# New numbers and a wider tie for TensorE in the list scheduler of a four-layer diffusion transformer step

## The chip, the core and the metric

The kernel runs on one core of a Trainium2 chip. The metric is the device time of one execution in microseconds (us); lower is better.

## What is computed

One inference step of a diffusion backbone: four layers on 128 context tokens and 512 latent tokens of width 1024, all in float32. Each layer takes one mixer: global attention (layers 0 and 3), windowed attention with a sink logit (layer 1), two-dimensional neighbourhood attention with a learned bias (layer 2). The reference, cut to what matters:

```python
for l in range(DEPTH):
    # the context tokens alike, with c_ctx in place of c and no positions
    shift, scl, gate = modulation(c, w_mod[l], b_mod[l])      # silu(c) @ w_mod + b_mod, 3 x 1024
    u = rms_norm(h_lat, norm_pre[l]) * (1 + scl[:, None, :]) + shift[:, None, :]
    q, k, v, z = project(u, w_in[l], q_norm[l], k_norm[l])    # 1024 -> 2560, q and k normed per head
    k_ctx, v_ctx = cache_k[:, l], cache_v[:, l]
    if kind == 0:
        q, k = apply_rope(q, cos, sin), apply_rope(k, cos, sin)
        o = dense_attention(q, concat(k, k_ctx), concat(v, v_ctx), None)
    elif kind == 1:
        q, k = apply_rope(q, cos, sin), apply_rope(k, cos, sin)
        o = window_attention(q, k, v, k_ctx, v_ctx, sink)
    else:
        o = neighborhood_attention(q, k, v, k_ctx, v_ctx, na_rel_bias[l // N_MIXERS])
    h_lat = h_lat + gate[:, None, :] * rms_norm((o * silu(z)) @ w_out[l], norm_post[l])
```

There are 16 query heads of 64 and 4 key heads; the reference returns both streams and the context keys and values of every layer.

## The kernel before, in words

**How the order comes about.** The program does not write instructions in their final order. It first records operations in program order (`S.op`): each has the engines that may do it with an estimated duration in ns, the buffers that it reads and writes, and a priority, which is its index in the program plus a shift for its part (the table `ORDER`; the modulation has its own shift). `Sched.emit` then plays these operations through a model of the engines and emits them one by one. Engines have letters: P is TensorE, V VectorE (DVE), A ScalarE (ACT), G GpSimd (POOL), D the DMA queue on SyncE (SP). For each engine `emit` takes every recorded operation whose inputs have been emitted, works out when it could start, and keeps the one with the lowest key:

```python
t = max(x[3], free[e] + (self.TURN.get((last, x[2][3]), 0) if e == "P" else 0))
key = (max(t, free[e] + SLACK[e]), x[0])
```

Here `x[3]` is the time at which the inputs are there, `free[e]` the time at which the engine is done, `x[0]` the priority. All operations that can start within `SLACK` of the engine's end are a tie, and the priority decides between them. Of the engines' candidates the one that starts first is emitted. The tables only set the order; the chip then runs each engine's instructions in that order, with semaphores between engines.

**Kinds of work on TensorE.** `TURN` adds ns to an operation of one kind behind one of another kind. M are ordinary matmuls: the projections in pieces of three matmuls (`nat`, L456, `z_block`, L593, `nat_o`, L860) and the scores (L657, L683, L759). T are float32 transposes: of the normed input (`start_part`, L410), of probabilities (L732, L785), and the two small matmuls of the modulation's fold (`mod_part`, L349). R are transposes in the float32r type (`k_stack`, L512, for the keys, called ks below; `q_chunk`, L579). C are matmuls with 64 columns, probabilities times values (L739, L793), and before the change also the modulation's matmuls with 32 columns (`mod_part`, L342).

**The modulation.** The 3072 columns of each later layer's modulation are worked out in pieces of 256 columns while the layer before runs. A piece loads two halves of `w_mod` of 512 KB each (L336, buffers `wm`, of which there are three), runs eight matmuls (L342), has the result copied by ACT or DVE (L252), and folds it on TensorE (L349). A buffer with one slot (`cap_mod`) lets one piece be between these steps at a time.

**Weights.** The projections' weights come as tiles of 256 KB (L318, three `raw` buffers), which ACT copies to a rounded half (L257) and DVE or POOL subtracts to a rest half (L258) in one of eight `w` buffers. All loads, the modulation's among them, go through SP's queue in the order of `emit`; the output phase reads the residual (L897, 512 KB) there, and layer 2 its bias table (L624, 132.5 KB a head).

**Layers.** A layer runs keys and values, two halves of the queries, the gate path and attention; then its output phase (L860) with the norm, and for each block of 128 tokens the next layer's input: square sum, power on POOL, scaling, transposes (L410), scale and shift on DVE or ACT, and the split into two halves for the next layer's first projection (L456).

## Time and profile before

| | us |
|---|---|
| median of 3 runs | 1426.93 |
| lowest and highest run | 1423.52, 1427.0 |
| the profiled execution | 1422.92 |
| its span from the first instruction to the last | 1420.7 |
| TensorE busy in it | 1381.5 |
| VectorE, ScalarE, GpSimd busy | 955.9, 755.7, 274.7 |

The profiled execution is the faster end of the runs. The rows that the argument uses stand in a section of their own below. In them a start is in us from the span's start; a row of the timeline joins neighbouring instructions of one line and tile (xcount), its second column is what they were busy for together, and a bracket at its end is the idle time ahead of it with what released it. Matmuls overlap a little, so a row's busy time reaches past the next row's start; the distance between two starts is what a row held the engine for. A float32 matmul that is no transpose leaves two records, so the eight matmuls of a modulation are 16 in the trace and the two of its fold 4.

### The profile page before, as it was taken

To read this page: it belongs to the slowest core of one execution; us is meant where nothing else is said; L and a number is where in the kernel's file an instruction comes from. 1 tells how busy PE (TensorE), PEld (TensorE's weight loads), DVE (VectorE), ACT (ScalarE), POOL (GpSimd) and SP (SyncE) were. 2 spreads that over 40 slices of the span, in tenths; PEclk is the share of its full clock that TensorE was granted. 3 is DMA by queue.
4 is the path that set the end of the run, shared out by engine and by line. 5 is a ranking of instruction groups with operands and counts; after the bars stand their busy time and mean duration, and the time that the engine had idled before them with its cause. 6 is when DMAs were issued, how large, how long until landed. Compare 5 with 4: busy or idle time off the path is not lost.

```text
span 1420.7 us, 24387 instructions
## 1 busy us (share of the span) xinstructions
PE 1381.5 (97%) x8964; PEld 1119.1 (79%) x8964; DVE 955.9 (67%) x2334; ACT 755.7 (53%) x1858; POOL 274.7 (19%) x322
## 2 busy tenths in 40 slices
PE   6999999999999999999999999999999999999998
PEld 4687878887777888877777887787787887888876
DVE  5777667775586875887287577558368776578654
ACT  4455554555354665567245458358345455655541
POOL 1231013010032101101022443155022210221100
PEclk9999999999999999999999999999999999999999
DMA  8513032125442212224444212233443210110043
GB/s 326 180 49 119 1 116 73 51 87 196 149 143 90 89 50 100 72 84 147 156 149 146 94 54 94 67 119 121 145 160 115 67 60 16 60 54 7 3 148 126
DMA packets 61799, 145.05 MB, mean 102 GB/s; under 512 B 7472, under 2 KB 12656, under 8 KB 61680
## 3 DMA queue, kind: packets, MB, share of 16 engines
q1 hardware_dynamic: 61680, 143.49, 30.6%
q8 instruction: 71, 1.16, 0.4%
q14 instruction: 48, 0.39, 0.1%
HBM read 131.90 MB, written 11.57 MB: 101 GB/s over the span
## 4 chain that ended last, share of the span: by engine, by line
PE 81%; DMA 5%; DVE 5%; ACT 3%; issue 3%; POOL 2%; SPq 0%; DVEq 0%; POOLq 0%; ACTq 0%
PE B L456 18%; PE B L593 14%; PE B L739 9%; PE B L732 9%; PE S L860 7%; PE B L860 5%; PE S L657 5%; PE S L683 4%; PE B L342 3%; DMA raw<-in_w_in 3%; DMA raw<-in_w_out 2%; POOL sm L303 2%; PE S L456 1%; PE B L579 1%; DVE w L258 1%
## 5 line engine op out<-in xcount | busy, mean ns | idle before, releaser
L303 POOL TENSOR_TENSOR sm<-sm,mhalf 128x1 f32<-128x1 f32 (+2 forms) x100 | 117.5, 1179 | 551.9 <-DVE sm L310 282.3
L456 PE MATMUL B<-w,uB 128*128 128x512 f32 x816 | 208.8, 401 | 1.5 <-DVE uB L258 1.1
L257 ACT ACTIVATE w<-raw 128x512 fp32r<-128x512 f32 x224 | 136.7, 627 | 93.0 <-DMA raw<-in_w_in 44.6
L252 ACT ACTIVATE pt<-B 128x512 f32<-128x512 f32 (+1 forms) x221 | 121.9, 569 | 110.7 <-PE B L732 102.5
L456 PEld LDWEIGHTS B<-w,uB 128*128 128x128 f32 x816 | 148.7, 188 | 35.1 <-DVE uB L258 1.6
L593 PE MATMUL B<-uB,w 128*128 128x384 f32 x768 | 166.1, 347 | 0.0
L732 PE MATMUL B<-ident,p 128*128 128x128 f32 x1088 | 159.4, 278 | 2.5 <-ACT pt L252 1.1
L258 DVE TENSOR_TENSOR w<-raw,w 128x512 fp32r<-128x512 f32 x187 | 128.1, 695 | 46.9 <-ACT w L257 46.0
L732 PEld LDWEIGHTS B<-ident,p 128*128 128x128 f32 x1088 | 123.0, 141 | 36.8 <-issue 25.1
L739 PE MATMUL B<-pt,vt 128*64 128x256 f32 (+1 forms) x1152 | 143.3, 377 | 0.0
L456 PE MATMUL B<-w,uA 128*128 128x512 f32 x528 | 134.3, 402 | 1.2 <-ACT w L257 0.5
L593 PEld LDWEIGHTS B<-uB,w 128*128 128x128 f32 x768 | 129.9, 189 | 1.3 <-issue 0.8
L662 ACT ACTIVATE p<-S,sm 128x640 f32<-128x640 f32 x128 | 101.0, 792 | 54.0 <-DVE sm L660 47.6
L660 DVE TENSOR_REDUCE sm<-S 128x1 f32<-128x640 f32 x128 | 102.1, 818 | 28.4 <-PE S L657 27.7
L593 PE MATMUL B<-uA,w 128*128 128x256 f32 x768 | 116.6, 290 | 3.8 <-ACT pt L252 2.4
L456 PEld LDWEIGHTS B<-w,uA 128*128 128x128 f32 x528 | 96.5, 188 | 24.7 <-DVE w L258 1.5
L617 POOL TENSOR_SCALAR p<-p,sm 128x640 f32<-128x640 f32 (+2 forms) x63 | 46.2, 738 | 353.4 <-DVE sm L616 268.4
L739 PEld LDWEIGHTS B<-pt,vt 128*64 128x64 f32 x1152 | 72.6, 136 | 47.6 <-issue 17.7
L593 PEld LDWEIGHTS B<-uA,w 128*128 128x128 f32 x768 | 103.6, 191 | 7.2 <-ACT pt L252 2.6
L617 DVE TENSOR_SCALAR p<-p,sm 128x640 f32<-128x640 f32 (+2 forms) x193 | 95.5, 512 | 5.8
L657 PE MATMUL S<-kst,q 128*128 128x320 f32 x512 | 95.6, 319 | 0.6 <-ACT p L662 0.6
L696 ACT ACTIVATE p<-p,sm 128x512 f32<-128x512 f32 (+1 forms) x128 | 84.0, 659 | 10.1 <-DVE sm L694 8.9
(143 smaller groups left out, 2255.3 us busy)
## 6 DMA issues: line engine op xcount, KB each, us to landing
raw<-in_w_in SPq DMA_DIRECT2D x160, 256.0 KB
wm<-in_w_mod SPq DMA_DIRECT2D x80, 512.0 KB
raw<-in_w_out SPq DMA_DIRECT2D x64, 256.0 KB
w<-in_w_mod SPq DMA_DIRECT2D x16, 512.0 KB
xs<-q SPq DMA_DIRECT2D x15, 512.0 KB
q<-xs SPq DMA_DIRECT2D x15, 512.0 KB
q<-in_x SPq DMA_DIRECT2D x10, 512.0 KB
kst<-gs SPq DMA_DIRECT2D x8, 512.0 KB
```

The costliest lines, as they stand in the source:

```text
L252: alts = {"A": Ap(n, lambda e: e.activation(out(), in_(), AF.Copy)), "V": V(n, lambda e: e.tensor_copy(out(), in_()))}
L257: S.op([As(n, lambda e: e.activation(h(), src(), AF.Copy))], r, w)
L258: f = lambda e: e.tensor_sub(l(), src(), h().bitcast(F32))
L303: S.op([("G", 395 + 157 * n, lambda e: e.tensor_tensor(r.ap, v.ap, mhalf.ap.to_broadcast([128, n]), op=OP.pow), "pow")], r=[v, mhalf], w=[r])
L456: e.matmul(ps(), t.ap[:, s, k, off:off + 128], W[k].ap[:, w], start=k == 0 and i == 0, stop=k == 7 and i == 2)
L593: e.matmul(ps.ap[:, 0:w], W[k].ap[:, wi, 128 * f:128 * f + 128], t.ap[:, s, k, :], start=k == 0 and i == 0, stop=k == 7 and i == 2)
L617: f = lambda e, i=i, p=p, w=w: e.tensor_scalar(p.ap[:, 0:w], p.ap[:, 0:w], rs.ap[:, i:i + 1], 1.0, op0=OP.mult, op1=OP.mult)
L657: e.matmul(ps.ap[:, b, 0:320], Q[t + 1].ap[:, hh], kst.ap[:, g, s, 320 * b:320 * b + 320], start=s == 0, stop=s == 1)
L660: S.op([V(640, lambda e, ps=ps, i=i: e.tensor_reduce(negm.ap[:, i:i + 1], ps.ap[:, :, 0:320], axis=AX.XY, op=OP.max, negate=True))], r=[ps ...
L732: e.transpose(pt.ap[:, c:c + 128], p.ap[:, b:b + 128], ident.ap)
L739: e.matmul(po.ap[64 * x:64 * x + 64, 256 * half + q0:256 * half + q0 + w], vt.ap[:, kt, 64 * g:64 * g + 64], sbt.ap[:, c0:c0 + w], start=f ...
L860: e.matmul(ps(), t.ap[:, s, k, off:off + 128], W[k].ap[:, w], start=k == 0 and i == 0, stop=k == 7 and i == 2)
```

## The change

The table `TURN` gets other numbers and more pairs, and the tie on TensorE grows from 30 to 100 ns. The modulation's matmuls become a kind of their own, E, whose pairs are priced like those of C, with 76 ns between C and E. C behind C, 30 before, costs nothing. Four durations in the model change: 960 to 935 for the modulation's matmuls, 260 to 448 for its fold, and 300 to 336 for the two float32r transposes. The model's numbers change nothing but the order in which operations are emitted, and which engine is given an operation that may go to several.

```diff
--- before.py
+++ after.py
@@ -33,7 +33,7 @@
 WINDOW = 520
 PLAT = 270
 XLAT = 180
-SLACK = {'P': 30, 'V': 0, 'A': 220, 'G': 50, 'D': 80}
+SLACK = {'P': 100, 'V': 0, 'A': 220, 'G': 50, 'D': 80}
 DISLIKE = {'Ap': 1060, 'mada': 3020, 'G1': 980, 'mad': 900, 'V': 1260, 'V2': 960, 'G': 780}
 CAPS = {'p': 6, 'raw': 3, 'cap_prep': 3}
 NEG = -1e30
@@ -63,7 +63,11 @@
     LAT = {("P", "P"): 0, ("V", "V"): 130, ("A", "A"): 155, ("G", "G"): 110, ("P", "V"): 200, ("P", "A"): 200,
            ("G", "V"): 80, ("A", "V"): 110, ("V", "A"): 135, ("G", "A"): 150, ("D", "D"): 100, ("V", "P"): 235, ("A", "P"): 228}
 
-    TURN = {("C", "M"): 85, ("C", "T"): 30, ("C", "R"): 30, ("C", "C"): 30, ("R", "M"): 52, ("R", "C"): 52}
+
+
+    TURN = {("C", "M"): 179, ("E", "M"): 179, ("C", "T"): 132, ("E", "T"): 132, ("C", "R"): 132, ("E", "R"): 132, ("R", "M"): 45,
+            ("R", "C"): 110, ("R", "E"): 110, ("R", "T"): 45, ("T", "M"): 6, ("M", "C"): 88, ("M", "E"): 88, ("T", "C"): 94,
+            ("T", "E"): 94, ("C", "E"): 76, ("E", "C"): 76}
 
 
 
@@ -341,13 +345,13 @@
                 g = 32 * (k % 4)
                 e.matmul(ps.ap[g:g + 32, 0:256], cpad.ap[:, k, :], raws[k // 4].ap[:, k % 4], start=k < 4, stop=k >= 4,
                          skip_group_check=True)
-        S.op([P(960, mm, "C")], r=raws + [cpad], w=[ps], touch=[cap])
+        S.op([P(935, mm, "E")], r=raws + [cpad], w=[ps], touch=[cap])
         evac(256, lambda: pm.ap, lambda: ps.ap[:, 0:256], [ps], [pm])
 
         def fold(e):
             for x in range(2):
                 e.matmul(ps.ap[:, 2 * x:2 * x + 2], pm.ap[:, 128 * x:128 * x + 128], sel.ap, start=True, stop=True)
-        S.op([P(260, fold, "T")], r=[pm, sel], w=[ps], touch=[cap])
+        S.op([P(448, fold, "T")], r=[pm, sel], w=[ps], touch=[cap])
         S.op([V(4, lambda e: e.tensor_tensor(mc.ap[:, b:b + 2], ps.ap[:, 0:4].rearrange("p (b j) -> p b j", j=2),
                                              bc.ap[:, b:b + 2, None].to_broadcast([128, 2, 2]), op=OP.add))],
              r=[ps, bc], w=[(mc, b), (mc, b + 1)], touch=[cap])
@@ -510,7 +514,7 @@
                 for g in range(2):
                     c = 128 * (2 * i + g)
                     e.transpose(ps.ap[:, c:c + 128], hl.ap[:, i, g].rearrange("p a d -> p (a d)"), identr.ap)
-        S.op([P(300, tr, "R")], r=[hl, identr], w=[ps], touch=tc_)
+        S.op([P(336, tr, "R")], r=[hl, identr], w=[ps], touch=tc_)
         evac(512, lambda: kst.ap[:, :, :, 128 * COL[ct]:128 * COL[ct] + 128],
              lambda: ps.ap.bitcast(F32).rearrange("p (i g c) -> p g i c", i=2, g=2), [ps], [(kst, ct)])
 
@@ -577,7 +581,7 @@
                 def tr(e, hl=hl, pt=pt):
                     for h in range(4):
                         e.transpose(pt.ap[:, 128 * h:128 * h + 128], hl.ap[:, h], identr.ap)
-                S.op([P(300, tr, "R")], r=[hl, identr], w=[pt], touch=[cap])
+                S.op([P(336, tr, "R")], r=[hl, identr], w=[pt], touch=[cap])
                 evac(512, lambda i=i, q=q: q.ap[:, 4 * i:4 * i + 4].rearrange("p h t -> p (h t)"),
                      lambda pt=pt: pt.ap.bitcast(F32), [pt], [(q, i)])
             Q.append(q)
```

The lines after the table move down by four (L342 is L346 afterwards, L739 is L743).

TensorE at the boundary of layers 0 and 1 (L456 is the last projections of the key phase, L410 the transposes of the last block of tokens, L512 the keys' transposes, L342 and L349 the modulation). Before:

```order
L349 MATMUL B<-sel,pm 128x2 x2
L456 MATMUL B<-w,uB 128x512 x3
L512 MATMUL B<-identr,tmp 128x128 x4
L456 MATMUL B<-w,uB 128x512 x6
L410 MATMUL B<-ident,p 128x128 x8
L512 MATMUL B<-identr,tmp 128x128 x4
L456 MATMUL B<-w,uB 128x512 x3
L342 MATMUL B<-wm,cpad 32x256 x8
L349 MATMUL B<-sel,pm 128x2 x2
L456 MATMUL B<-w,uB 128x512 x24
```

After, in the same place:

```order
L516 MATMUL B<-identr,tmp 128x128 x4
L460 MATMUL B<-w,uB 128x512 x3
L516 MATMUL B<-identr,tmp 128x128 x4
L460 MATMUL B<-w,uB 128x512 x3
L346 MATMUL B<-wm,cpad 32x256 x8
L414 MATMUL B<-ident,p 128x128 x8
L353 MATMUL B<-sel,pm 128x2 x2
L516 MATMUL B<-identr,tmp 128x128 x4
L460 MATMUL B<-w,uB 128x512 x6
L516 MATMUL B<-identr,tmp 128x128 x4
L460 MATMUL B<-w,uB 128x512 x18
```

The modulation's eight matmuls, which stood behind the eight L410 transposes, now stand ahead of the same transposes (L414), three of the matmuls of L456 with them; behind the transposes a fold and one keys' transpose are left ahead of the long run of matmuls.

TensorE in the attention of layer 1, second half of the queries (L683 scores, L732 transposes of probabilities, L739 probabilities times values). Before:

```order
L739 MATMUL B<-pt,vt 64x256 x6
L739 MATMUL B<-pt,vt 64x128 x2
L732 MATMUL B<-ident,p 128x128 x4
L593 MATMUL B<-uB,w 128x384 x6
L683 MATMUL S<-kst,q 128x384 x2
L683 MATMUL S<-kst,q 128x512 x2
L683 MATMUL S<-kst,q 128x256 x4
L683 MATMUL S<-kst,q 128x384 x2
L732 MATMUL B<-ident,p 128x128 x14
L739 MATMUL B<-pt,vt 64x256 x6
L739 MATMUL B<-pt,vt 64x128 x2
L342 MATMUL B<-wm,cpad 32x256 x8
```

After:

```order
L743 MATMUL B<-pt,vt 64x256 x2
L743 MATMUL B<-pt,vt 64x128 x2
L346 MATMUL B<-wm,cpad 32x256 x8
L736 MATMUL B<-ident,p 128x128 x4
L687 MATMUL S<-kst,q 128x384 x2
L687 MATMUL S<-kst,q 128x512 x2
L736 MATMUL B<-ident,p 128x128 x7
L687 MATMUL S<-kst,q 128x256 x4
L687 MATMUL S<-kst,q 128x384 x2
L353 MATMUL B<-sel,pm 128x2 x2
L743 MATMUL B<-pt,vt 64x256 x4
L346 MATMUL B<-wm,cpad 32x256 x8
```

Before, a modulation stands at the end of the stretch behind a group of L739. After, two stand in it, each behind such a group, with 11 transposes, 10 score matmuls, a fold and four matmuls of L743 between them.

SP's queue at the boundary of layers 1 and 2 (raw<-in_w_out are tiles of the output projection, q<-xs the residual, tab the bias table of layer 2). Before:

```order
L318 DMA raw<-in_w_out 128x512 x3
L897 DMA q<-xs_4216 128x1x1024 x2
L318 DMA raw<-in_w_out 128x512 x2
L624 DMA tab<-in_na 128x1x265
L318 DMA raw<-in_w_in 128x512 x3
```

After:

```order
L322 DMA raw<-in_w_out 128x512 x3
L628 DMA tab<-in_na 128x1x265 x2
L901 DMA q<-xs_4225 128x1x1024
L322 DMA raw<-in_w_out 128x512 x2
L322 DMA raw<-in_w_in 128x512
L901 DMA q<-xs_4225 128x1x1024
L322 DMA raw<-in_w_in 128x512 x2
```

Two loads of the bias table and one of the residual now stand ahead of the last two tiles of the output projection, where two of the residual stood; the second residual load has moved behind them.

## Rows read from the trace of the kernel before

**Rows 1.** The page: busy time by engine, clock in 40 slices, chain by engine.

```profile
PE 1381.5 (97%) x8964; PEld 1119.1 (79%) x8964; DVE 955.9 (67%) x2334; ACT 755.7 (53%) x1858; POOL 274.7 (19%) x322
...
PEclk9999999999999999999999999999999999999999
...
PE 81%; DMA 5%; DVE 5%; ACT 3%; issue 3%; POOL 2%; SPq 0%; DVEq 0%; POOLq 0%; ACTq 0%
```

**Rows 2.** Timeline of PE, five places: start, busy us, engine, line, out<-in, shapes, count.

```profile
451.92 5.84 PE L456 MATMUL B<-w,uB 128*128 128x512 f32 x24
457.60 0.80 PE L579 MATMUL B<-identr,tmp 128*128 128x128 f32 x8
...
489.69 1.73 PE L739 MATMUL B<-pt,vt 128*64 128x256 f32 x16
491.36 0.65 PE L732 MATMUL B<-ident,p 128*128 128x128 f32 x4
...
637.49 0.87 PE L739 MATMUL B<-pt,vt 128*64 128x256 f32 x8
638.29 0.66 PE L732 MATMUL B<-ident,p 128*128 128x128 f32 x4
...
658.25 1.08 PE L739 MATMUL B<-pt,vt 128*64 128x256 f32 x8
659.26 0.55 PE L732 MATMUL B<-ident,p 128*128 128x128 f32 x3
...
1355.93 3.08 PE L860 MATMUL S<-w,uB 128*128 128x512 f32 x12
1358.94 0.66 PE L793 MATMUL B<-pt,vt 128*64 128x128 f32 x8
```

**Rows 3.** Timelines of SP (988.65) and PE (993.15) in layer 2.

```profile
988.65 0.39 SPq L336 DMA_DIRECT2D wm<-in_w_mod  x1
...
993.15 0.64 PE L342 MATMUL B<-wm,cpad 128*32 128x256 f32 x8 [0.26 <-DMA wm<-in_w_mod]
```

**Rows 4.** Timelines of SP and PE; windows (busy by engine, PEclk, DMA share, GB/s).

```profile
691.02 1.74 SPq L318 DMA_DIRECT2D raw<-in_w_out  x3
692.80 1.23 SPq L897 DMA_DIRECT2D q<-xs  x2
696.54 1.03 SPq L318 DMA_DIRECT2D raw<-in_w_out  x2
...
705.76 0.50 PE L860 MATMUL B<-w,uA 128*128 128x512 f32 x1 [2.42 <-ACT w L257]
706.49 5.08 PE L860 MATMUL B<-w,uA 128*128 128x512 f32 x14 [0.23 <-DVE w L258]
...
697.00:699.00 2.00, 1.87 (x7) 0.99 (x6) 0.77 (x3) 0.63 (x1) 0.00 (x0) 1.00 0.75 237
...
707.00:709.00 2.00, 2.00 (x6) 1.61 (x5) 0.05 (x1) 0.09 (x1) 0.00 (x0) 0.50 0.67 214
```

**Rows 5.** Timeline of PE at the first two boundaries between layers.

```profile
426.99 1.03 PE L410 MATMUL B<-ident,p 128*128 128x128 f32 x8
...
429.01 1.07 PE L342 MATMUL B<-wm,cpad 128*32 128x256 f32 x16
430.59 0.61 PE L349 MATMUL B<-sel,pm 128*128 128x2 f32 x4 [0.51 <-ACT pm L252]
431.05 2.11 PE L456 MATMUL B<-w,uB 128*128 128x512 f32 x8
...
763.28 1.07 PE L342 MATMUL B<-wm,cpad 128*32 128x256 f32 x16
```

**Rows 6.** Timeline of PE: waits in layers 0 and 2.

```profile
193.83 1.20 PE L512 MATMUL B<-identr,tmp 128*128 128x128 f32 x12 [1.12 <-ACT tmp L503]
...
884.72 0.66 PE L785 MATMUL B<-ident,p 128*128 128x128 f32 x4 [0.41 <-ACT pt L252]
...
887.62 0.96 PE L456 MATMUL B<-w,uA 128*128 128x512 f32 x3 [0.31 <-DVE tmp L469]
```

## The prediction

> **What bounds the kernel now.** First the busy times of the whole execution, the granted clock in 40 slices and the chain of waits [rows 1]: TensorE is busy for 1381.5 of 1420.7 us, so at most 39.2 us of the span is TensorE standing still, and the granted clock shows full speed in every slice. The chain that ended last goes through TensorE for 81%. So two things can move the time: what TensorE pays for its own work, and those 39 us. The pitch of the work shows that "busy" is not a trick of overlapping records: 24 matmuls of L456 in a row go from 451.92 to 457.60, 237 ns each, and that pitch recurs in every long run [rows 2]. The Trainium skill ("Perfetto Trace Analysis", section "Identifying the Most-Contended Engine") says that matmul busy share tells little of the headroom, and that the busy share of weight loads is the measure. That share is 79% here [rows 1]; by the rule a fifth of the span would be free, dearer or cheaper switches would be hidden, and the first term below would be 0, the sum -1.3. The pitch speaks against it, and I go by the pitch.
>
> **What the change does to the order.** The computation and the number of instructions on TensorE stay; the order moves. Counted over all rows of the two orders, TensorE enters a group of C or E matmuls (L739, L793, L342; neighbours counted as one group) 151 times before and 147 times after; runs of transposes fall from 285 to 268. More visible is where the E groups (modulation, L342) go. With the new table an E costs 76 ns behind a C, inside the tie of 100, while a transpose or an ordinary matmul costs 132 or 179 and falls out of it. So nearly every E is taken behind a C group as soon as its weights count as landed, up to 90 us earlier than before in the attention phases, and the ones left for the phases between layers become fewer. On SP the w_mod loads move with them, and at the second layer boundary other loads are exchanged.
>
> **Term 1, switches.** Two rows give a price. Twelve matmuls of L860 between two C groups take 3.01 us (1355.93 to 1358.94), twelve of L456 without one 2.84 (half of 5.68): 0.17 for leaving one C and entering the next [rows 2]. A C group's own time: 8 alone take 0.80 and 1.01 (637.49 to 638.29, 658.25 to 659.26), 16 together 1.67 (489.69 to 491.36), so joining two saves 0.14 [rows 2]. Together 0.31 us a group, against 0.22 to 0.27 in the table of the diff. Four groups fewer are -1.2 by the rows; all kinds of switches, count times the diff's numbers, give -1.07. I take **-1.1**, bounds -0.8 and -1.3. That is the whole direct gain: the count hardly falls, because entering a C (88) now also lies inside the tie.
>
> **Term 2, wider ties.** With a tie of 100 ns instead of 30, TensorE may be given an operation whose data come later although another stands ready. Run over the planner's choices this happens 20 times after and 9 before, so 11 more, each at most 100 ns: 0 to +1.1, I take **+0.5**, the middle.
>
> **Term 3, E behind its own load.** An E needs two 512 KB loads; three buffers exist, so the second load can only start when the E before it is done. At 988.65 SP issued such a second load amid weight loads, and the half of the E that needs it began at 993.15 after 0.26 idle: 4.5 us from issue to use [rows 3]. In the new order the distance from the E that frees the buffer to the E that needs it, priced with the start-to-start times of the same operations in this trace, is some 4.5 and 4.7 us in two places (the order of the attention phase of layer 1 shows the first) and 6.4 to 8 in six more; before, all but that one were 8.5 or more. The nearest row is the one at 988.65, a load of the same size in traffic: two waits of a quarter, **+0.5**. Lower bound 0; upper bound from the slowest landing in the rows, the loads issued at 696.54 whose tile is used at 705.76 [rows 4]: 9.2 us less the tile's conversion, which would be some 4 us of waiting at each of the two tightest: +8.
>
> **Term 4, the load that comes late at 705.** TensorE stands for 2.42 us at 705.76 on the ACT half of a w_out tile, and then runs at half clock (0.50, the 1.2 GHz level, from 707 to 709) [rows 4]. The 14 matmuls from 706.49 on are busy for 5.08 us, where 14 x 0.237 = 3.32 would do, and the one ahead of them holds the engine for 0.73 instead of 0.24: together 2.2 more, so the place costs 4.6. The two late loads were issued at 696.54 behind three of 256 KB and two of 512 KB: 1792 KB. In the new order one of the 512 KB loads stands behind them, and two of 132.5 KB in front: 1545 KB. At the 237 GB/s of 697 to 699 [rows 4] the 247 KB are 1.0 us. The wait would then be about 1.4 us, and a wait of 1.12 at 193.83 was not followed by the half clock [rows 6], so most of the 2.2 goes too: **-3.0**. Bounds 0 (the queue drains no earlier) and -4.6 (the place goes).
>
> **Term 5, fillers lost at the layer boundaries.** At 426.99 eight transposes start, whose result comes back through DVE for the matmuls at 431.05. Between them lie a ks transpose, three matmuls, an E (1.0 us with its half-microsecond wait behind it, 0.51 idle) and its fold, 0.46 [rows 5]. In the new order only a fold and a ks transpose stand there; the E comes 50 us later. If the way through DVE stays as long, the matmuls start when they did, and 1.0 + 0.46 of work is still owed. At the next boundary the same pattern holds one E of 1.0, at 763.28, which also goes. **+2.5**. Below: +1, if the three matmuls now ahead of the transposes fill time that was idle before them. Above: each of the two new waits comes near the 2.42 of term 4 and is followed by half clock for 2 us: +6.5.
>
> **Term 6, E in front of waits.** Several waits in the attention phases were TensorE arriving early: 1.12 at 193.83 (ACT), 0.41 at 884.72 and 0.31 at 887.62 [rows 6]. In front of each, two to four more E groups now stand, so TensorE arrives 3 to 5 us later while ACT and DVE get little new work: **-1.8**. Bounds -1.8 and 0, where the waits travel along because what they wait for also follows from TensorE's work.
>
> **Sum.** -1.1 + 0.5 + 0.5 - 3.0 + 2.5 - 1.8 = -2.4 us. The profiled execution took 1422.9 us (span 1420.7 and 2.2 around it), 4.0 below the median of the runs, 1426.93. Against its own time the sum gives 1420.5; set against the median, which the result will be compared with, 1424.5.
>
> **Rivals.** *Faster.* The wait at 705 goes with its half clock (-4.6), the early arrivals go and their smaller kin with them (-3), the boundaries lose one filler's worth (+1); with terms 1 and 2 (-0.6) that is -7.2, 1419.7. For it: all of these are short waits with an explanation in the order. Against it: freed waits on a shared ACT and DVE often reappear at the next exchange. *Slower by lost fillers.* Both boundary waits reach about 2 us, half clock follows each (+6.5), the 705 place stays as it is, term 6 gives 1: with the rest +5.4, 1432.3. It decides at the wait behind the eight transposes: waits of 1.12 left the clock alone, 2.42 did not. For it: the two new waits are estimated at just 2 us, and lost fillers are visible in the order. Against it: three matmuls have moved in front of the transposes and DVE may answer sooner. *Slower by late E weights.* If loads in traffic take 6.5 us instead of 4.5, the two tight places and those at 6.4 to 6.6 wait, some 4 us, and weight loads queued behind them on SP slip too: with +2 for that, some +5.5 on the rest without term 3's half, 1429 to 1433, 1432. *No effect.* If "busy by weight loads" were right or the waits simply change places, 1426.9.
>
> **How the numbers follow.** Forecast 0.33 (its own range 1422.6 to 1429); no effect 0.05; faster 0.34; slower by lost fillers 0.17; slower by late weights 0.11. A measurement of this kernel can tell about 0.3%, 4.3 us, from no change; so faster 0.34, same 0.38, slower 0.28. Faster and slower together hold more than half, so the range takes both in: 1417 leaves out the lower third of the faster case, 1434.5 the upper part of the slower ones.
>
> **What the profile after would show.** Term 1: L739 rows still in some 130 runs, E behind L739 in about two thirds. Term 3: waits of TensorE at L342 (now L346) on wm loads, under 1 us in all; several us mean the late-weights rival. Term 4: the wait of a w_out matmul at the second boundary under 1.5 us and no slice of half clock there. Term 5: idle time of about 2 us behind the L410 (now L414) transposes at two boundaries; a granted clock of 0.5 behind them is the fillers' rival. Term 6: no wait of over 0.5 us at the ks transposes near 194. The prediction is wrong if waits of TensorE on weight tiles (w from ACT or DVE) grow by several us in places that none of these terms names.

## The result and the profile after

The changed kernel is slower: a median of 1434.75 us over 5 runs (1432.86 to 1436.9), against 1426.93 over 5 runs of the kernel before (1423.52 to 1428.57). The ratio is 1.0070, with an interval from 1.0046 to 1.0093, so 7 to 13 us; the two medians are 7.8 apart. The forecast was 1424.5, and the end of its range, 1434.5, lies just below the result. The profiled execution is the one of 1434.75, with a span of 1433.0; the one of before had 1420.7, so there are 12.3 us to find between the two traces.

The page of the changed kernel, busy times and the chain that ended last, to be read against [rows 1]:

```profile
PE 1386.2 (97%) x8964; PEld 1122.6 (78%) x8964; DVE 963.4 (67%) x2340; ACT 756.0 (53%) x1855; POOL 268.0 (19%) x319
...
PE 80%; DVE 6%; DMA 6%; issue 4%; ACT 3%; POOL 1%; SPq 0%; DVEq 0%; POOLq 0%; ACTq 0%
```

The busy time of TensorE grew by 4.7 us though it has the same 8964 instructions, and its idle time from 39.2 to 46.8. Part of "busy" is half clock, so a finer account is needed. For it, each operation of TensorE is given the distance to the next one that the trace of before usually shows for its kind and the kinds of its neighbours; what a trace has beyond that is **standing or half clock**. It is an estimate, worked out from the two traces. By it the new order needs 1.1 us less in pure work, and 13.4 more of standing and half clock (62.1 against 48.7). Where it lies, in us, with the stretches in times of the trace of before (each begins and ends where both orders have issued the same work; the first 6 us are left out):

| stretch | before | after | after less before |
|---|---|---|---|
| 6 to 392: start, layer 0 | 23.4 | 21.7 | -1.7 |
| 392 to 496: first layer boundary | 2.7 | 4.3 | +1.6 |
| 496 to 665: layer 1 | 1.2 | 1.6 | +0.3 |
| 665 to 751: output phase of layer 1 | 8.7 | 11.4 | +2.7 |
| 751 to 825: second boundary, projections | 0.0 | 6.0 | +6.0 |
| 825 to 1005: layer 2 | 2.2 | 6.5 | +4.3 |
| 1005 to the end | 10.5 | 10.6 | +0.1 |

The traces say the same without any account. At places where both orders have issued exactly the same work on TensorE, the changed kernel is 2.1 us ahead at 392 and 0.7 ahead at 510, level at 724, and behind by 3.4 at 754, 8.3 at 825 and 12.0 at 1005.

TensorE between 695 and 772 in the changed kernel (timeline; a bracket is the idle time ahead and what ended it):

```profile
707.47 0.49 PE L864 MATMUL B<-w,uA 128*128 128x512 f32 x1 [3.03 <-ACT w L261]
708.20 4.98 PE L864 MATMUL B<-w,uA 128*128 128x512 f32 x14 [0.23 <-DVE w L262]
...
737.32 0.49 PE L460 MATMUL B<-w,uA 128*128 128x512 f32 x1 [3.42 <-ACT w L261]
...
757.05 0.52 PE L516 MATMUL B<-identr,tmp 128*128 128x128 f32 x4 [0.91 <-DVE tmp L426]
...
766.99 0.54 PE L516 MATMUL B<-identr,tmp 128*128 128x128 f32 x4 [0.68 <-DVE tmp L426]
...
769.53 2.08 PE L460 MATMUL B<-w,uB 128*128 128x512 f32 x4 [1.14 <-DVE uB L262]
```

The first wait is that of [rows 4], 3.03 instead of 2.42, again with 14 matmuls in 4.98 us behind it; between 510 and 724, where it lies, the two traces differ by no more than 0.7. The second is new: a tile of the next layer's w_in, 3.42. The three waits below are at the second boundary, where before had none of over 0.2 after 748.

SP and ACT of the changed kernel show how late the two tiles are: the issue on SP, and the conversion on ACT, which waits for the load.

```profile
693.27 1.73 SPq L322 DMA_DIRECT2D raw<-in_w_out  x3
695.05 1.30 SPq L628 DMA_DIRECT2D tab<-in_na  x2
696.39 0.58 SPq L901 DMA_DIRECT2D q<-xs  x1
698.79 0.99 SPq L322 DMA_DIRECT2D raw<-in_w_out  x2
...
726.29 0.61 SPq L922 DMA_DIRECT2D xs<-q  x1
...
728.07 4.01 SPq L322 DMA_DIRECT2D raw<-in_w_in  x3
...
706.79 1.28 ACT L261 ACTIVATE w<-raw 128x512 fp32r<-128x512 f32 x2 [7.79 <-DMA raw<-in_w_out]
...
736.64 1.67 ACT L261 ACTIVATE w<-raw 128x512 fp32r<-128x512 f32 x3 [6.66 <-DMA raw<-in_w_in]
```

The w_out tile issued at 698.79 is converted at 706.79, 8.0 us later; the w_in tile issued at 728.07 at 736.64, 8.6 us later. In the kernel before the same w_in tile was issued at 728.98, and ACT, which was busy with other work from 731.45 on, took it at 732.08.

### The profile page after: what moved, and what is told of

It reads as the page before. It is cut to its first block, busy times and chain, and to the rows that moved or that the text cites. A ratio compares the mean times of both kernels' runs of the same rounds, so it can differ in the third digit from the quotient of the medians.

```text
span 1433.0 us, 24375 instructions
## 1 busy us (share of the span) xinstructions
PE 1386.2 (97%) x8964; PEld 1122.6 (78%) x8964; DVE 963.4 (67%) x2340; ACT 756.0 (53%) x1855; POOL 268.0 (19%) x319
## 4 chain that ended last, share of the span: by engine, by line
PE 80%; DVE 6%; DMA 6%; issue 4%; ACT 3%; POOL 1%; SPq 0%; DVEq 0%; POOLq 0%; ACTq 0%
PE B L460 20%; PE B L597 13%; PE B L736 8%; PE B L743 8%; PE S L864 7%; PE B L864 5%; PE S L661 5%; PE S L687 3%; DMA raw<-in_w_in 3%; PE B L346 2%; DMA raw<-in_w_out 2%; PE B L583 2%; DVE w L262 1%; DVE tmp L426 1%; ACT w L261 1%
## 5 line engine op out<-in xcount | busy, mean ns | idle before, releaser
L256 ACT ACTIVATE pt<-B 128x512 f32<-128x512 f32 (+1 forms) x216 | 118.9, 567 | 102.0 <-PE B L736 98.1
L262 DVE TENSOR_TENSOR w<-raw,w 128x512 fp32r<-128x512 f32 x196 | 135.1, 700 | 52.9 <-ACT w L261 51.9
L743 PE MATMUL B<-pt,vt 128*64 128x256 f32 (+1 forms) x1152 | 144.0, 377 | 0.0
L666 ACT ACTIVATE p<-S,sm 128x640 f32<-128x640 f32 x128 | 101.2, 794 | 70.9 <-DVE sm L664 59.0
L621 POOL TENSOR_SCALAR p<-p,sm 128x640 f32<-128x640 f32 (+2 forms) x73 | 53.2, 735 | 397.3 <-DVE sm L620 282.8
L743 PEld LDWEIGHTS B<-pt,vt 128*64 128x64 f32 x1152 | 73.1, 136 | 46.3 <-issue 16.0
L621 DVE TENSOR_SCALAR p<-p,sm 128x640 f32<-128x640 f32 (+2 forms) x183 | 91.6, 515 | 5.1
L700 ACT ACTIVATE p<-p,sm 128x512 f32<-128x512 f32 (+1 forms) x128 | 84.0, 658 | 12.6 <-DVE sm L698 10.6
```

The lines of the kernel that those rows point to most:

```text
L256: alts = {"A": Ap(n, lambda e: e.activation(out(), in_(), AF.Copy)), "V": V(n, lambda e: e.tensor_copy(out(), in_()))}
L262: f = lambda e: e.tensor_sub(l(), src(), h().bitcast(F32))
L621: f = lambda e, i=i, p=p, w=w: e.tensor_scalar(p.ap[:, 0:w], p.ap[:, 0:w], rs.ap[:, i:i + 1], 1.0, op0=OP.mult, op1=OP.mult)
L743: e.matmul(po.ap[64 * x:64 * x + 64, 256 * half + q0:256 * half + q0 + w], vt.ap[:, kt, 64 * g:64 * g + 64], sbt.ap[:, c0:c0 + w], start=f ...
```

## Experiments

Ratios are against runs of the kernel before on the same chip; 0.001 is 1.43 us. Where an order is spliced or moved, the kernel replays a fixed list of operations, taken from the `emit` of one of the two kernels or of both, and the diff shows the list or the rows of one engine. An operation that the two orders have on different sides of a cut is fitted in so that each is issued once. Where two ratios from different chips are compared, their difference is known to some 0.002 to 0.003, 3 to 4 us; a smaller gain is one only if the trace shows it too.

### The second boundary, put in and taken out

```diff
-PLAN = before
+PLAN = before[:3229] + after[3229:3882] + before[3882:]
```

> The order of the kernel before, except the stretch of the second layer boundary (about 675 to 828 us), where the order of the changed kernel stands. Theory (the loss lies in what stands in this stretch: the wait of 3.03 for a w_out tile, the wait of 3.42 for a w_in tile with its half clock, the waits behind the L410 transposes; together +8.0 us between the two traces): 1426.9 + 8 = 1434.9. Rival (the stretch is only where a delay surfaces that the order ahead of it, in the attention of layer 1, has caused): about 1427, within 1.5.

Measured: 1432.89, ratio 1.0054 (1.0034 to 1.0074), 7.7 us. The theory stands: this stretch alone makes most of the loss. In the profiled execution, the fastest of the four, the wait for the w_in tile is 1.19 and not 3.42.

```diff
-PLAN = after
+PLAN = after[:3229] + before[3229:3882] + after[3882:]
```

> The mirror of it: the order of the changed kernel, except that stretch, where the order of the kernel before stands. Theory of the stretch: 1434.75 - 8 = 1426.7, with the second loss, in the attention of layer 2 (+4.1 between 828 and 1005 us), still there. Rival: about 1434.5, the waits appear at the same place in another order of the same work.

Measured: 1430.06, ratio 1.0025 (1.0007 to 1.0043), that is 6.4 us better than the changed kernel, nearer the theory's 8 than the rival's 0. But the wait for the w_out tile, which the order of before has too, was longer in the profiled execution, the slowest of ten, than in [rows 4], 5.25:

```profile
714.20 6.48 PE L864 MATMUL B<-w,uA 128*128 128x512 f32 x15 [5.25 <-ACT w L261]
```

So a late load is no fixed number: with the same rows of SP ahead of it the tile took 8.5 us from issue to conversion in the kernel before and 10.2 here (703.28 to 713.52). The rest of the longer wait is TensorE's, which has 1.1 us less to do between issue and wait than in the kernel before, as in the changed kernel (term 4 below).

### Where the modulation stands

```diff
-PLAN = before
+PLAN = before, its modulation operations behind the neighbours that they have in after
```

> The order of the kernel before for everything but the modulation, whose loads, matmuls, copies and folds stand where the changed kernel has them. Theory M (where the modulation stands is the cause: fillers lost at two boundaries, 1.6 and 3.5, and a PSUM bank held for long in layer 2, 3.4): 1426.9 + 8.5 = 1435. Rival (the rest of the order, that is the ties among transposes, projections and loads, is the cause): 1427, or 1426 by the switches saved.

```diff
-PLAN = after
+PLAN = after, its modulation operations behind the neighbours that they have in before
```

> The mirror: the order of the changed kernel for everything but the modulation, which stands where the kernel before has it. Theory M: 1434.75 - 8.5 = 1426.3, with the late w_in load of the second boundary (some 4) still there or not according to how SP's queue falls. Rival: 1434 to 1435.

Measured: 1454.64, ratio 1.0204 (1.0183 to 1.0225), and 1462.51, ratio 1.0262 (1.0230 to 1.0294). Both fall far outside either theory. The waits of TensorE in the first of the two (us in total, times, longest):

```profile
PE B L736 <- DVE modc L355: 3.7, 13, 0.3
```

Transposes now wait 13 times for the last step of a modulation (L355), and folds 8 times for their copy. The two halves of an order were made for each other; mixed, they cost 29 and 37 us. This says nothing on which half causes the loss, but it shows how much one consistent order is worth.

### The two late tiles, one move on SP each

The store behind the three w_in loads (rows of SP):

```diff
 xs<-q x1
-xs<-q x1
 raw<-in_w_in x3
+xs<-q x1
 raw<-in_w_in x3
```

> The order of the changed kernel with one move: the 512 KB store of the residual stream that SP issues at 726.29 stands behind the three w_in loads that follow it (728.07 to 731.75). Theory T (the loads land late because the store is ahead of them in the DMA engines: 8.2 us from issue to landing, where the same load took under 3.1 in the kernel before, with no store ahead): the wait of 3.42 at 737 and its half clock go, 1434.75 - 4.2 = 1430.5. Rival (a weight load takes some 8 us at such a place whatever is ahead of it): no change, 1434.75, wait still over 3.

Measured: 1432.64, ratio 1.0042 (1.0025 to 1.0059). Against 1.0070 that is 4.0 us of the expected 4.2, about what the two intervals leave undecided; the trace shows it more plainly. The same tile is issued at the same point of TensorE's work and is converted 3.1 us later (726.44 to 729.53) instead of 8.6. The wait for the w_in tile is gone from the trace; that for the w_out tile stays:

```profile
707.28 0.49 PE L864 MATMUL B<-w,uA 128*128 128x512 f32 x1 [2.48 <-ACT w L261]
708.01 3.54 PE L864 MATMUL B<-w,uA 128*128 128x512 f32 x14 [0.23 <-DVE w L262]
```

The bias tables and the residual behind the two w_out tiles:

```diff
 raw<-in_w_out x3
-tab<-in_na x2
-q<-xs x1
 raw<-in_w_out x2
+tab<-in_na x2
+q<-xs x1
 raw<-in_w_in x1
```

> The order of the changed kernel with one move: the two 132.5 KB bias tables and the 512 KB of the residual, which SP issues from 695.05 to 696.39, stand behind the two w_out tiles of 698.79. Theory T: the wait of 3.03 at 707.47 and its half clock go, 1434.75 - 5.2 = 1429.5. Rival: no change, 1434.75, the wait still over 2.

Measured: 1431.62, ratio 1.0030 (1.0010 to 1.0050), 5.7 us of the expected 5.2. The w_out wait is gone; 1.10 of the w_in wait is left, at 727.49.

The kernel before with the same idea, its two residual loads behind the two w_out tiles:

```diff
 raw<-in_w_out x3
-q<-xs x2
 raw<-in_w_out x2
+q<-xs x2
 tab<-in_na x1
```

> The order of the kernel before with one move: the two 512 KB loads of the residual that SP issues at 692.80 and 693.46 stand behind the two w_out tiles of 696.54. Theory T (late landing by the traffic ahead): the tiles land in some 3.5 us, the wait of 2.42 at 705.76 and the half clock behind it go, 1426.25 - 4.6 = 1421.7. Rival (the tiles land late anyway, since they are issued when the raw buffers come free and the queue holds other loads): 1426, the wait still over 2.

Measured: 1418.34, ratio 0.9943 (0.9925 to 0.9962), faster than both kernels. Timelines of SP and TensorE:

```profile
694.60 6.46 SPq L318 DMA_DIRECT2D raw<-in_w_out  x5
701.11 1.24 SPq L897 DMA_DIRECT2D q<-xs  x2
...
702.40 7.76 PE L860 MATMUL B<-w,uA 128*128 128x512 f32 x32 [0.17 <-DVE w L258]
```

Five tiles go out first, and 32 matmuls run through with 0.17 of idle time. Theory T holds in all three: a 256 KB tile is late because of what SP issued ahead of it, and a transfer that is needed 30 us later may stand behind it (the moved residual, issued at 701.11, is first read at 731.94).

Both moves on the changed kernel (the two diffs above together):

> The order of the changed kernel with both moves on SP: the store of the residual stream behind the three w_in loads, and the bias tables and the residual behind the two w_out tiles. Theory T (two loads that land late, each for itself): the gains of the two moves add, 2.1 and 3.1, 1434.75 - 5.2 = 1429.5, with no wait of over 0.5 on a weight tile between 700 and 750. Rival (one move already shifts the other load out of the traffic): 1431.6, as with the tables alone.

Measured: 1425.73, ratio 1.0006 (0.9991 to 1.0020), 9.1 us better than the changed kernel. The two gains add (4.0 and 5.7), so the rival falls. TensorE's waits for weight tiles between 700 and 750 are gone:

```profile
696.14 11.40 PE L864 MATMUL B<-w,uA 128*128 128x512 f32 x48
```

The changed kernel is now level with the kernel before. But the kernel before gained from the same cure, so between the two orders with their queues mended some 7 us are left (1.0006 against 0.9943, and against 0.9967 in the second comparison below).

### The wide tie alone

```diff
-SLACK = {'P': 30, 'V': 0, 'A': 220, 'G': 50, 'D': 80}
+SLACK = {'P': 100, 'V': 0, 'A': 220, 'G': 50, 'D': 80}
```

> The kernel before with the tie on TensorE at 100 ns, the table and the durations as before. The order then enters groups of C matmuls 168 times, where the kernel before does it 151 and the changed kernel 147 times. Theory S (a switch costs what the rows of before gave, 0.22 to 0.31 us a group): 17 more are +4 to +5, 1430.5 to 1431.5, if the waits stay. Rival (the wide tie brings the loss, whatever the table): 1434 or more. Rival (neither switches nor ties matter): 1426.

Measured: 1436.67, ratio 1.0081 (1.0056 to 1.0106). By the account of the first section the trace is 19.3 us longer than that of before, 14.1 of it standing and half clock and **5.2 pure work, 0.31 for each of the 17 more entries**. That is the price of a switch in term 1, as far as the account can tell it, and the table of the change does what it says: with the old table the wide tie adds entries, with the new one it loses four. The waits come on top, the longest at the w_out tile again. The counterpart, the new table with the old tie, was not tried, so what the table does alone is not shown.

The same kernel with the residual loads moved:

```diff
 raw<-in_w_out x3
-q<-xs x2
 raw<-in_w_out x2
+q<-xs x2
 raw<-in_w_in x1
```

> The kernel before with the tie at 100 ns alone, and the two residual loads moved behind the two w_out tiles. Theory T (the wide tie loses at the late w_out tile, a wait of 5.94 and what follows it): 1436.7 - 8 = 1428.7, of which 4 to 5 over the kernel before with the same move (1418.3) are the 17 more entries into C groups and the rest other waits. Rival (the wide tie loses all along the way): 1434 or more.

Measured: 1442.16, ratio 1.0118 (1.0097 to 1.0139), slower still. Ahead of the move and behind it (tie_only, then tie_queue):

```profile
714.61 6.76 PE L860 MATMUL B<-w,uA 128*128 128x512 f32 x21 [5.94 <-ACT w L257]
```

```profile
705.51 0.63 SPq L336 DMA_DIRECT2D wm<-in_w_mod  x1
...
719.89 1.08 PE L342 MATMUL B<-wm,cpad 128*32 128x256 f32 x8 [5.88 <-DMA wm<-in_w_mod]
```

The wait of 5.94 for the tile became one of 5.88 for a modulation's weights. Their load stands behind the residual in both orders (issued at 704.38 in tie_only and, as far as the buffers tell, at 705.51 here); but without the wait for the tile TensorE comes to that modulation at 713.37 instead of 721.31, and then the load is late. Theory T is not wrong on the tile, but a move on a queue only helps if the next load in it is in time as well.

### What is left: TensorE's fillers, VectorE's order, the stretches

TensorE's rows at the second boundary of the changed kernel, the other engines as they were:

```diff
-L516 x4
 L460 x6
+L516 x4
...
-L346 x8
 L414 x8
-L353 x2
+L346 x8
 L516 x4
+L353 x2
```

> The order of the changed kernel with two moves on TensorE at the second layer boundary: the keys' transposes that wait 0.91 at 757.05 stand behind the next six matmuls of L460, and the modulation's matmuls of 763.88 stand behind the eight L414 transposes and not ahead of them (its fold behind the keys' transposes). No other engine's order changes. Theory F (fillers: the way of the transposes through DVE has a fixed length, and what is ready should stand behind them): 0.9 and 1.0 us, 1434.75 - 1.9 = 1432.9, and of the 5.1 us of standing and half clock that the stretch from 751 to 795 has in the trace of the changed kernel some 3.2 are left. Rival (the waits travel along behind what is moved): 1434.75, still 5 in the stretch.

Measured: 1435.37, ratio 1.0081 (1.0061 to 1.0102), no gain. The rows of TensorE:

```profile
760.30 1.64 PE L460 MATMUL B<-w,uB 128*128 128x512 f32 x6 [0.93 <-DVE tmp L426]
...
769.80 0.51 PE L516 MATMUL B<-identr,tmp 128*128 128x128 f32 x4 [0.70 <-DVE tmp L426]
...
772.25 2.08 PE L460 MATMUL B<-w,uB 128*128 128x512 f32 x4 [0.95 <-DVE uB L262]
```

The wait of 0.91 ahead of the keys' transposes (L516) is now one of 0.93 ahead of the matmuls, for the same release (L426 reads the transposes out of PSUM). The waits of 0.68 and 1.14 behind the L414 transposes are 0.70 and 0.95, with the modulation between them; the same work, from its first row to the start of the matmuls that wait, took 5.65 us before the moves (763.88 to 769.53) and 5.18 with them (767.07 to 772.25). So of the forecast 1.9 some 0.5 came in the trace, and none in the time. VectorE shows why, in the changed kernel and then with the moves:

```profile
765.57 1.36 DVE L426 TENSOR_SCALAR tmp<-B,modc 128x128 f32<-128x128 f32 x4 [0.55 <-PE B L414]
...
768.79 1.29 DVE L262 TENSOR_TENSOR uB<-tmp,uB 128x512 fp32r<-128x512 f32 x2
```

```profile
768.30 1.36 DVE L426 TENSOR_SCALAR tmp<-B,modc 128x128 f32<-128x128 f32 x4
...
771.52 1.28 DVE L262 TENSOR_TENSOR uB<-tmp,uB 128x512 fp32r<-128x512 f32 x2
```

From the first L426 to the L262 that frees the matmuls it works through without a gap, 3.9 us in both. With the moves the transposes come sooner in the order, but VectorE is still at other work and begins on them 1.23 us after their start (767.07) instead of 0.69 (764.88). Two moved fillers do not return the loss. That says nothing against the larger number of them in the old order, which has nine and 24 matmuls of L456 and a modulation behind the same transposes, none of which waits.

On VectorE, with SP mended:

```diff
+L426 x4
 L262 x1
-L426 x4
...
+L262 x1
 L426 x4
 L497 x1
-L262 x2
+L262 x1
```

> The order of the kernel with both moves on SP's queue, with two more moves on VectorE alone, at the second layer boundary: the scale and shift of the transposes (L426) of 744.75 stands ahead of the subtraction (L262) that was ahead of it, so the PSUM bank for which the keys' transposes wait 1.37 at 746.26 comes free sooner; and the subtraction that the matmuls of L460 wait 1.15 for at 758.74 stands ahead of the second L426. TensorE's order is unchanged. Theory D (VectorE's order sets the pace of this boundary, not what stands on TensorE): some 0.8 and 1.1 us, 1425.7 - 1.9 = 1423.8, and of the 4.3 us of standing and half clock between 740 and 782 some 2.4 are left. Rival (the waits travel along, as they did when TensorE's instructions were moved): 1425.7, still over 4 in the stretch.

Measured: 1426.38, ratio 1.0005 (0.9990 to 1.0021), the same as without. The rows of TensorE:

```profile
746.99 0.51 PE L516 MATMUL B<-identr,tmp 128*128 128x128 f32 x4 [0.83 <-DVE tmp L426]
747.92 4.45 PE L460 MATMUL B<-w,uB 128*128 128x512 f32 x18 [0.42 <-DVE tmp L473]
...
761.17 0.36 PE L516 MATMUL B<-identr,tmp 128*128 128x128 f32 x2 [1.04 <-ACT tmp L507]
```

The 1.37 became 0.83 + 0.42; the 1.15 for the subtraction is gone, and 1.04 stands two rows later for the keys' split. Again the wait travels. VectorE is full here in both orders; in the old one TensorE has other work meanwhile (windows of the changed kernel, then of the kernel before; busy of PE, PEld, DVE, ACT and POOL, clock, DMA share, GB/s):

```profile
767.00:769.00 2.00, 1.27 (x6) 0.69 (x6) 2.00 (x7) 1.59 (x3) 0.00 (x0) 1.00 0.84 328
769.00:771.00 2.00, 1.47 (x4) 1.18 (x5) 1.65 (x5) 1.34 (x4) 0.00 (x0) 0.61 0.03 12
```

```profile
761.00:763.00 2.00, 2.00 (x12) 1.60 (x10) 2.00 (x7) 1.23 (x2) 0.00 (x0) 1.00 0.11 45
```

Whole stretches taken back, first layer 2:

```diff
-PLAN = after
+PLAN = after[:3882] + before[3882:4899] + after[4899:]
```

> The order of the changed kernel, except from 828 to 1005 us (attention of layer 2), where the order of the kernel before stands. Theory B (modulation pieces that stand early hold a PSUM bank for 8 to 13 us, so transposes wait for banks, as at 880.95 and 899.22): the difference of the traces in this stretch, 4.1, comes back, 1434.75 - 4.1 = 1430.7. Rival (these waits come and go between executions of one order): 1434, at most 1.5 less.

Measured: 1430.89, ratio 1.0051 (1.0033 to 1.0068), 2.7 us better than the changed kernel, between theory and rival and within what the two intervals leave open. What theory B means stands in the trace of the changed kernel:

```profile
873.34 1.07 PE L346 MATMUL B<-wm,cpad 128*32 128x256 f32 x16
...
880.95 0.55 PE L736 MATMUL B<-ident,p 128*128 128x128 f32 x3 [1.32 <-DVE gate L605]
...
886.26 0.14 DVE L355 TENSOR_TENSOR modc<-B,bcol 128x4 f32<-128x4 f32 x1
```

The modulation that starts at 873.34 holds one of the four PSUM buffers until its last step at 886.26, 13 us; in the kernel before, the one at 868.84 held its buffer for 6.5. Another buffer is with the gate path until L605, which is what the transposes at 880.95 wait for. But that wait of 1.32 stands in this trace alone of the eight that have the new order here (two others have 0.3 there). In queue_both the same modulation holds its buffer for 11.5 us (861.11 to 872.62), and nothing waits for L605. What recurs in all eight are these waits, 2.7 us in all, where the eight of the old order have 1.0 to 2.4 of others (waits of queue_both from 826 to 1020: total, times, longest):

```profile
PE B L516 <- ACT kst L256: 1.0, 2, 0.7
PE B L736 <- DVE p L621: 0.6, 1, 0.6
PE B L583 <- DVE tmp L578: 0.5, 1, 0.5
PE B L736 <- DVE modc L355: 0.4, 1, 0.4
PE B L516 <- DVE tmp L473: 0.2, 1, 0.2
```

Only 0.4 of it is a wait for a modulation's last step (L355). A held buffer leaves three for the others, so it may have a part in the rest; no run shows it. So theory B is not shown beyond that 0.4.

```diff
-PLAN = after, with both moves on SP
+PLAN = the same, with before[3882:4899] in place of after[3882:4899]
```

> The order of the changed kernel with both moves on SP's queue, and from 828 to 1005 us the order of the kernel before. Theory A (the losses add): 1425.7 - 3.9 = 1421.8. Rival: 1425.7, at most 1 less; in the trace with both moves the wait of 880.95 has no counterpart.

Measured: 1425.86, ratio 1.0001 (0.9985 to 1.0016), 0.7 us better than 1.0006: the rival, as far as medians can tell. In the traces the stretch is 1.2 us shorter (181.2 against 182.4).

```diff
-PLAN = after, with the tables and the residual moved on SP
+PLAN = the same, with before[3364:3882] in place of after[3364:3882]
```

> The order of the changed kernel with the bias tables and the residual behind the two w_out tiles, and from about 721 to 828 us the order of the kernel before (in which the store stands behind the loads). Theory A (the losses add: the queue's, the boundary's own 4 us between 740 and 795, layer 2's): 1425.7 - 4 = 1421.7. Rival (with the late loads gone the rest of the boundary hides behind other work): 1425.7.

Measured: 1422.99, ratio 0.9987 (0.9973 to 1.0001), 2.7 us of the expected 4. The stretch from 724 to 825 takes 2.5 us less than in queue_both (99.8 against 102.3), but the one ahead of it, from 510 to 724, takes 1.4 more.

Because single waits come and go, the stretches were compared over all executions that had either order there. Plain time in us between places where both orders have issued the same work on TensorE, means (lowest to highest, number of executions). ready_first counts only outside the second boundary; with SP mended the new order is that of queue_both, queue_layer2 and dve_order, and in the old one SP needs no mending between 724 and 825:

| stretch | order of before | order of the changed kernel |
|---|---|---|
| first boundary, 392 to 510 | 118.4 (117.8 to 119.4, 6) | 120.8 (119.5 to 121.9, 10) |
| 510 to 724, SP mended | 209.2 (209.0 to 209.5, 3) | 209.6 (209.3 to 209.9, 3) |
| second boundary, 724 to 825, SP mended | 100.3 (99.6 to 101.2, 7) | 103.1 (102.3 to 103.9, 3) |
| layer 2, 825 to 1005 | 180.7 (179.9 to 181.8, 8) | 182.9 (182.4 to 183.9, 8) |

In three of the four the two orders' executions don't overlap.

All three stretches taken back at once:

```diff
-PLAN = after, with the tables and the residual moved on SP
+PLAN = the same, with before[:2274], [3364:3882] and [3882:4899] behind after[:1683] and after[:3364]
```

> The order of the changed kernel with the bias tables and the residual behind the two w_out tiles, and the order of the kernel before in three stretches: 383 to 502 us (first layer boundary), 721 to 828 (second) and 828 to 1005 (layer 2). Theory A (the traces of the two orders, each with its queue mended, differ by 3.1 at the first boundary, 3.4 at the second, 2.5 in layer 2 and 1.4 in layer 3, less 1.1 for switches, and these add): what is left is layer 3's 1.4, so within 1.5 of the kernel before with its residual loads moved, about 1419. Rival (the loss is spread over the whole order or comes and goes): 1422 or more.

> The kernel before with the two residual loads behind the two w_out tiles once more, on the same chip as the run beside it, for a comparison of like with like. Theory T: 0.994 of the kernel before, as at first (1418.3 against 1426.0). Rival (the first result was the chip's): 1.000.

Measured, side by side: 1420.44, ratio 0.9960 (0.9949 to 0.9972), and 1420.04, ratio 0.9967 (0.9951 to 0.9983). Theory A holds: without those three stretches the new order is level with the old one. The first boundary was not taken back by itself, so its share rests on the traces. The kernel before with its residual loads moved stays the fastest, 0.9943 and 0.9967 in its two comparisons.

One more version, the kernel before with the residual moved and the new order from 78 to 383 us, where the trace of the changed kernel lacks the wait of 1.83 at 111.46:

```diff
-PLAN = before, with the residual moved on SP
+PLAN = before[:376] + after[376:1683] + the same from there on
```

> The kernel before with the residual loads moved as in the earlier run, and from 78 to 383 us the order of the changed kernel, whose trace is 2.3 us ahead there (the wait of 1.83 at 111.46 is gone). Theory (the gain is the order's): 1418.3 - 2.3 = 1416. Rival (the wait at 111 comes and goes between executions): 1418.

Measured: 1418.84, ratio 0.9964 (0.9948 to 0.9980), no better than 0.9943 and 0.9967: the rival. That wait is an execution's, not the order's; it is 0.36 in the trace of boundary_in, which has the old order there.

## Why the prediction was wrong, by its own steps

Two steps failed: term 4, which took a late load as a matter of bytes at one place (-3.0 forecast, +2.7 measured), and term 6, which gave the moved modulation no cost (-1.8 forecast, +2.2 measured in layer 2). Term 5 came out at twice its size (+2.5 forecast, +5.2 measured).

**Term 1, switches, -1.1:** right in size. By the account the new order's pure work is 1.1 less, and the 17 additional entries of tie_only cost 0.31 each, the price that [rows 2] gave. The Trainium skill ("Perfetto Trace Analysis", section "Identifying the Most-Contended Engine") judges TensorE's headroom by MFU, the share of peak arithmetic, and by the busy share of weight loads. From the second alone the prediction read that switches would be hidden, set the pitch against it and went by the pitch. The runs agree with the pitch: in tie_only, at a weight-load share of 78%, the 17 entries show up as 5.2 us of work by the account.

**Term 2, ties, +0.5:** no run tells it apart. Outside the stretches of terms 4 to 6 the two traces differ by 1.7 and less, no more than executions of one order do.

**Term 3, modulation behind its own load, +0.5:** nothing came; no wait on a wm load stands in the changed kernel's trace. The mechanism is real, as the 5.88 of tie_queue shows, but there the load was late, not the distance short.

**Term 4, the late tile at 705, -3.0:** wrong. It counted the bytes ahead of the load, 247 KB fewer, as 1.0 us, and took for granted that TensorE would come to the tile as late as before. TensorE, before and then after:

```profile
683.06 11.41 PE L860 MATMUL S<-w,uA 128*128 128x512 f32 x48
...
696.41 0.50 PE L349 MATMUL B<-sel,pm 128*128 128x2 f32 x4
...
699.10 4.24 PE L860 MATMUL B<-w,uA 128*128 128x512 f32 x17 [0.23 <-DVE w L258]
```

```profile
685.31 11.40 PE L864 MATMUL S<-w,uA 128*128 128x512 f32 x48
...
696.55 7.89 PE L864 MATMUL B<-w,uA 128*128 128x512 f32 x33
```

Counted from the start of the 48 matmuls, the tiles are issued after 13.48 us in both. They are converted 0.5 sooner than before (8.0 us behind the issue instead of 8.5), half of the forecast. But TensorE runs out of work 1.15 sooner (704.44 less 685.31, against 703.34 less 683.06): the fold (0.36) and some 0.7 lost at an earlier tile (699.10) no longer stand in between. So the wait grew to 3.03, though the matmul that waits starts 0.5 sooner, counted from the 48; where -3.0 was forecast, the place gained half a us. With the tile of the next paragraph, late tiles cost the new order some 2.7 us more than the old one (9.1 against 6.4, below).

The same step looked only at the place where a late load was known. The new order put a 512 KB store ahead of the next w_in loads, and a second late tile, worth 4.0 by store_later, appeared at 737. Growing waits on weight tiles in places that no term names were the case in which the prediction called itself wrong. A bound of +4 to +5 for another late load should have been in the sum, since the order of SP showed that store moving.

**Term 5, the layer boundaries, +2.5:** the sign and the places are right, the size is half of what came, and the mechanism is shown in part. With SP mended on both sides the first boundary takes 2.4 more and the second 2.8, 5.2 together, within the bounds of +1 and +6.5. The rows at the first boundary, 0.87 ahead of the transposes and 0.77 and 1.14 behind them where [rows 5] had 0.51:

```profile
424.65 1.06 PE L414 MATMUL B<-ident,p 128*128 128x128 f32 x8 [0.87 <-ACT tmp L507]
426.83 0.50 PE L516 MATMUL B<-identr,tmp 128*128 128x128 f32 x4 [0.77 <-DVE tmp L426]
429.28 1.20 PE L460 MATMUL B<-w,uB 128*128 128x512 f32 x4 [1.14 <-DVE uB L262]
```

The idle time of about 2 us behind the transposes, which the prediction named as its sign, is there: 0.77 + 1.14 at the first boundary and 0.68 + 1.14 at the second. What it left out are the waits ahead of the transposes, 0.87 and 0.91, and the clock: it took the half clock to need a wait of about 2 us, and at the second boundary the granted clock fell to 0.61 behind these shorter ones. Whether lost fillers make the idle time is not settled: two of them put back at the second boundary (ready_first) returned 0.5 us of 1.9 there and nothing in the time, and another order on VectorE (dve_order) only moved the waits. What the runs show is that the old order, on all engines together, has no wait of 0.2 or more between 752 and 825, in times of the trace of before, in seven executions, and the new order has the same three in its seven: for L426 (1.6 to 2.9 in all), for L262 (1.1) and for the queries (L578, 0.5). Which of its exchanges is at fault stays open.

**Term 6, modulation ahead of waits, -1.8:** wrong in sign. The waits that it named did shrink: that of 1.12 at 193.83 to one of 0.28, and those of 0.41 and 0.31 are not among the new order's. But in layer 2 others came, 2.7 us of them in every trace of the new order, and the stretch takes 2.2 more on average instead of less. The step asked whether TensorE arrives later, not what else the moved operations hold up until their last step. What makes the new waits is not shown, except for the 0.4 at L355.

**The sum.** The rival "slower by lost fillers" came nearest, 1432.3, and it is partly luck: it had the waits behind the transposes, and half clock behind the second, but it kept the 705 place as it was and named no second late tile.

**What makes the loss**, with the orders compared like with like: +2.4 at the first boundary, +0.4 and +2.8 up to the end of the second, +2.2 in layer 2, together 7.8 us, switches included. The two kernels with SP mended differ by 0.0051 in ratio (1.0006 less 0.9955, the mean of the two comparisons), 7.3 us. As they stand, each order has its late tiles besides, worth 9.1 us in the new one and 6.4 in the old one, 2.7 more. That makes 10.5, where the ratio says 7 to 13.

## What to carry to other kernels

On a queue that many loads share, look at what stands ahead of the load that the busiest engine waits for next, and let transfers that are needed 30 us later go behind it; two moved rows gave 5 to 8 us here, more than the change was worth in switches. A wait is the load's time less the work that TensorE has meanwhile, so moving work away from a late load lengthens the wait as surely as a longer queue does: 1.15 us of it here. Before moving work into gaps, list what it holds (a PSUM buffer, a load buffer, a place in a queue) from its first to its last step; in mod_after transposes waited 13 times for it. A better table in a scheduler's cost model buys what it prices, here 1 us, and shuffles all that it doesn't price: judge the new order by its waits at the exchanges, over several executions, not by the number that was mended.

## What the runs showed that was not expected

The clock does not follow from the length of a wait alone. Behind 2.42 us of idle time in the kernel before the granted clock fell to 0.50 [rows 4], and behind 3.03 in the changed kernel too; behind 2.48 in store_later, at the same matmul, it stayed at full speed. Windows of the changed kernel, of store_later, and of queue_both at its first boundary:

```profile
708.00:710.00 2.00, 1.80 (x4) 1.49 (x5) 0.80 (x2) 0.07 (x1) 0.00 (x0) 0.50 0.63 179
```

```profile
708.00:710.00 2.00, 1.99 (x9) 1.60 (x10) 0.60 (x1) 0.52 (x2) 0.00 (x0) 1.00 0.74 241
```

```profile
426.00:428.00 2.00, 1.10 (x3) 0.50 (x2) 2.00 (x6) 1.00 (x3) 0.00 (x0) 0.50 0.00 0
```

The same 14 matmuls took 5.08 us behind 2.42, 4.98 behind 3.03 and 3.54 behind 2.48, so a wait of about 2.4 us may cost 1.5 more or nothing. Nor are short waits safe: in queue_both the clock fell to 0.50 amid waits of 0.87, 0.77 and 0.90 at the first boundary, where the changed kernel, with 0.87, 0.77 and 1.14 at the same rows, kept full speed.

A 256 KB tile took 6.3 to 11.1 us from issue to conversion behind a 512 KB store or a mix of loads (boundary_in and tie_only have the ends), and 3.1 with nothing ahead. And one order's executions differ by 3 to 4 us at the start alone: the stretch from 6 to 88 us has 13.1 to 18.4 of standing over the traces looked at.
